# Two edits to a two-layer attention trunk: where 64-query products stand in the first layer, and how many rows the second layer's rotary low-part product uses

## The chip, the core and the metric

The kernel runs on one core of a Trainium2 chip. The metric is the device time of one execution in microseconds (us); lower is better. Three runs of the kernel before took 1453.0, 1454.13 and 1455.13 us, a median of 1454.13 us. A profile of one execution stands beside them.

The engines are named as in the profile: PE is TensorE's matmul, PEld its weight load, DVE is VectorE, ACT is ScalarE, POOL is GpSimd, SP is SyncE, which issues the weight transfers.

## What is computed

The input is x with 256 tokens of 2048 elements, float32. Two layers follow each other, each `x <- LayerNorm(alpha * x + out_proj(mixer(x) * silu(z)))`.

- Layer 1 mixes with three groups of 16 heads of 128 dims. Group 0 is a causal band over the last 128 tokens. Groups 1 and 2 attend with strides 4 and 16. Queries and keys carry rotary embeddings, and the three groups share one softmax.
- Layer 2 is latent attention: queries and keys/values come from latents of rank 512. Each of 16 heads has scores from two parts, a 128-dim part of its own and a 64-dim rotary part whose key is shared by all heads: `s = q_nope . k_nope + q_pe . k_pe`, causal, then softmax and values.

## The kernel before, in words

**Precision.** Most products run on operands split in two float32r parts, hi and lo, with lo = x - hi. `mm3` (lines 294 to 299) adds three products into one accumulator: hi by hi (L297), hi by lo (L298) and lo by hi (L299). The split of the weights is ACT's copy on L174 (`whi`) and DVE's subtraction on L175 (`wlo`), from tiles `raw` that SP loads on L155. Each weight block is used for 256 tokens and never again; four `whi` and four `wlo` half-blocks and three `raw` blocks are in flight. The large projections, tile `acc`, are the bulk of all matmuls.

**Order.** The loop bodies give a list of projection steps, and `run_slots` puts attention tasks behind given steps. The tile framework's planner then fixes the order on each engine, from a simulated timeline: where an instruction is not ready in that simulation, later work in program order is put in front of it. The order on each engine is fixed when the kernel is built.

**Layer 1.** Eight pairs of heads; each has 20 projection steps of 24 matmuls. In each, `scores(p, h)` runs for two heads, h = 0 behind step 13 and h = 1 behind step 15. For each of two query blocks qb of 128 queries it takes a PSUM tile `t`, fills columns 0 to 255 with group 0's scores by `mm3` (128 queries by 256 keys), and columns 256 to 383 with groups 1 and 2: tokens are permuted so that each class of 64 tokens attends within itself, so these are four products of 64 queries by 64 keys, in plain float32, each on the 64 output partitions of its class (L439). Each float32 product shows as two records. Then `softmax` (L357 to L360) runs on DVE and ACT over the tile, and `turn_p` transposes it some steps later. `qf`, the operand of L439, is copied out of PSUM by ACT on L404, after the transposes behind step 12.

**Layer 2.** Four quads of four heads. `scores_b(c, h)` fills one PSUM tile per head with the scores of both query blocks, 128 keys for the first and 256 for the second (`SEG`). For each block it issues `mm3` on the 128-dim parts and then two rotary products. The rotary operands are laid on both halves of the partitions: `qp` holds q's hi part on partitions 0 to 63 and its lo part on 64 to 127, and both `kp[0]` (hi) and `kp[1]` (lo) hold the same 64 rows of the key twice. L751 multiplies all 128 rows of `qp` with `kp[0]`, which gives (q hi + q lo) by k hi; L752 multiplies rows 0 to 63 alone with `kp[1]`, which gives q hi by k lo. Softmax follows on DVE and ACT, and `turn_pb` transposes the probabilities on L761 in a later task.

Of the kernel before, what the change touches and what calls it, by code (L numbers as in the profile page):

```python
# [38 lines left out]
SUB = 4          # k tiles of 128 that share one step of a wide projection chunk  # L39
CAP = SUB * 512  # elements per partition of one weight block  # L40

# token order of the first layer's attention: p = (t % 4) * 64 + (t % 16) // 4 * 16 + t // 16
# [3 lines left out]
class Plan:  # L46
    """The order in which weight blocks are stored and used. A block is [128, kts, n]."""
# [6 lines left out]
    def add(self, kts, n, pick):  # L54
        """pick(weights) gives the block's [kts * 128, n] columns."""
        self.blocks.append((self.size, kts, n))
        self.make.append(pick)
        self.size += P * kts * n
        return len(self.blocks) - 1
# [70 lines left out]
def trunk(ctx: ExitStack, tc: tile.TileContext, plan, ids, wall, xt, x, pos, freqs, mask_a, mask_b, rmst, ln, out):  # L130
    nc = tc.nc
# [12 lines left out]
    # ---------------------------------------------------------------- weights, in order of use  # L144
# [50 lines left out]
    # ---------------------------------------------------------------- x, transposed  # L195
# [17 lines left out]
    # ---------------------------------------------------------------- constants  # L213
# [20 lines left out]
    def rope_tables():  # L234
        pt = const.tile([P, 4], I32, name="pt")
        nc.gpsimd.dma_start(pt, pos)
        fr = const.tile([P, NA + NB], F32, name="fr")
        nc.gpsimd.dma_start(fr, bass.AP(tensor=freqs.tensor, offset=freqs.offset, ap=[[0, P], [1, NA + NB]]))
        with tc.tile_pool(name="tab", bufs=1) as tab:
            pf = tab.tile([P, 4], F32, name="pf")  # L240
            nc.vector.tensor_copy(pf, pt)
            ang = tab.tile([P, NT], F32, name="ang")
            part = tab.tile([P, 2, NT], F32R, name="part")
            acc = tab.tile([P, 2, NT], F32, name="acc")
            rd = tab.tile([P, 2, NT], F32, name="rd")
            for i, (a, n, f) in enumerate(((0, NA, 0), (NA, NA, 0), (2 * NA, NB, NA), (2 * NA + NB, NB, NA))):
                nc.vector.tensor_scalar(ang[:, a:a + n], fr[:, f:f + n], pf[:, i:i + 1], None, op0=ALU.mult)
            nc.vector.tensor_copy(part[:, 0], ang)
            nc.vector.tensor_sub(part[:, 1], ang, f32(part[:, 0]))

            def fraction(dst, src):
                """dst = src less the nearest whole number"""
                r = rd if len(src.shape) == 3 else rd[:, 0]
                nc.vector.tensor_scalar(r, src, MAGIC, None, op0=ALU.add)
                nc.vector.tensor_scalar(r, r, MAGIC, None, op0=ALU.subtract)
                nc.vector.tensor_sub(dst, src, r)

            # angle / (2 pi) in parts of 12 bits, each product exact and reduced to its fraction of a turn
            turn = [0x28BE60DB9391054A, 0x7F09D5F47D4D3770]
            bits = (turn[0] << 64) | turn[1]  # 1 / (2 pi) as a binary fraction of 128 bits  # L260
            cs = [float(bits >> (128 - 14)) * 2.0 ** -14]
            for i in range(1, 5):
                cs.append(float((bits >> (128 - 12 * (i + 1) - 2)) & 0xFFF) * 2.0 ** (-12 * (i + 1) - 2))
            for i, c in enumerate(cs):
                if i < 3:
                    pr = acc if i == 0 else tab.tile([P, 2, NT], F32, name="pr", tag="pr")
                    nc.vector.tensor_scalar(pr, f32(part), c, None, op0=ALU.mult)
                    fraction(pr, pr)
                    if i:
                        nc.vector.tensor_add(acc, acc, pr)  # L270
                else:  # under half a turn for any int32 position
                    nc.vector.scalar_tensor_tensor(acc, f32(part), c, acc, op0=ALU.mult, op1=ALU.add)
            si = acc[:, 0]
            nc.vector.tensor_add(si, si, acc[:, 1])
            fraction(si, si)
            co = acc[:, 1]
            nc.vector.tensor_scalar(co, si, 0.25, None, op0=ALU.add)
            fraction(co, co)
            w = 6.283185
            av = lambda t: t[:, :2 * NA].rearrange("p (t n) -> p t n", n=NA)  # L280
            bv = lambda t: t[:, 2 * NA:].rearrange("p (t n) -> p t n", n=NB)
            for v, c_t, s_t in ((av, cosA, sinA), (bv, cosB, sinB)):
                nc.scalar.activation(c_t, v(co), AF.Sin, scale=w)
                nc.scalar.activation(s_t[:, :, 1], v(si), AF.Sin, scale=w)
                nc.vector.tensor_scalar(s_t[:, :, 0], s_t[:, :, 1], -1.0, None, op0=ALU.mult)

    # ---------------------------------------------------------------- shared pieces
# [6 lines left out]
    def mm3(o, a, b, start, stop):  # L294
        """o += a.T @ b for operands in two exact parts; the parts' product lo x lo is below float32."""
# [9 lines left out]
    def power(dst, src, mul, eps):  # L305
        """dst = (src * mul + eps) ** -0.5"""
        nc.gpsimd.tensor_scalar(dst, src, mul, eps, op0=ALU.mult, op1=ALU.add)
        nc.gpsimd.tensor_tensor(dst, dst, mhalf.to_broadcast(list(dst.shape)), op=ALU.pow)

    def slots_wide(name, n, src, total=KT, step=SUB, tb_outer=False, evac=None):  # L310
        """One projection chunk: token-major [128 tokens, n] for both token blocks, as a list of steps."""
# [26 lines left out]
    def rope(dst, src, heads, half, c_t, s_t, tmp):  # L338
        """dst = rope(src) for src [128, heads, 2, half] in PSUM; tables [128, half] and [128, 2, half]."""
# [7 lines left out]
    def silu(dst, e):  # L347
        """dst = dst / (1 + e), e = exp(-dst), not before the weights that were split last"""
# [5 lines left out]
    def softmax(dst, src, mask, scale, sums, tmp):  # L354
        """dst = exp(scale * (src + mask) - max), sums = its row sums."""
# [8 lines left out]
    def run_slots(slots, todo):  # L364
        """Interleave: after step i the tasks todo[i]."""
# [5 lines left out]
    # ---------------------------------------------------------------- layer A: dilated windows  # L371
# [3 lines left out]
    def layer_a():  # L375
# [30 lines left out]
        def evac_v(p, part):  # L406
            def f(tb, acc):
                if part == 0 and tb == 0:
                    # group 0's values; groups 1 and 2's side by side for each class of tokens (t % 4)
# [17 lines left out]
        def scores(p, h):  # L427
            qh, ql, qf = pair[p, "q"]
            if h == 0:
                pair[p, "s"] = ap.tile([P, 2, 2, 384], F32, name="s", tag="s")  # L430
                pair[p, "sum"] = ap.tile([P, 4], F32, name="sum", tag="sum", bufs=2)
            for qb in range(2):
                t = at_tile()
                q = slice(qb * P, (qb + 1) * P)
                mm3(t[:, 0:256], (qh[:, h, q], ql[:, h, q]), (qh[:, 2 + h], ql[:, 2 + h]), True, True)
                for c in range(2):
                    for g in range(2):
                        q = slice(qb * P + 64 * c, qb * P + 64 * c + 64)
                        nc.tensor.matmul(t[64 * c:64 * c + 64, 256 + 64 * g:320 + 64 * g], qf[:, g, h, q], qf[:, g, 2 + h, q],  # L439
                                         start=True, stop=True)  # L440
                i = 2 * h + qb
                softmax(pair[p, "s"][:, h, qb], t[:, 0:384], mask[:, qb], SCALE_A, pair[p, "sum"][:, i:i + 1], ap)
# [31 lines left out]
        def values(p, h):  # L474
# [12 lines left out]
            def nat(a):  # tokens back in their own order  # L487
# [38 lines left out]
    # ---------------------------------------------------------------- output projection and LayerNorm  # L526
    def norm(v, mean, rstd, shift, gb, mul):
        """v = (v - mean) * rstd * g + b, on the vector engine alone or on three with mul for the product"""
# [8 lines left out]
    def norm_rows(layer):  # L537
        """the layer's g and b for each quarter of a row, on every partition"""
# [8 lines left out]
    def out_layer(tag, todo, res, u, whole):  # L547
        """u = ALPHA * res + y @ w_out; whole(tb, q, mean, rstd, -mean * rstd) ends a quarter of a token block's row.
        The last 8 steps are token block 0's last columns and then token block 1's."""
# [18 lines left out]
        # blocks are stored in the order 0.0 1.0 0.1 1.1 0.2 1.2 0.3 1.3  # L568
# [33 lines left out]
    # the first steps of the output projection finish the last heads  # L602
# [4 lines left out]
    # ---------------------------------------------------------------- layer B: latent attention  # L607
# [4 lines left out]
    shared = []  # one wide tile: first the latents, then gates' exponentials and values  # L612
# [64 lines left out]
    def heads_t(name, key, c, lat, parts_tag):  # L677
        """[128 dims, 4 heads, 256 tokens] in parts, weights stationary."""
# [33 lines left out]
    def turn_qp(c):  # L712
        """each head's rotary queries, [hi; lo] on the two halves of the partitions"""
# [25 lines left out]
    SEG = ((0, 128), (128, 256))  # columns of a head's scores, by query block  # L739

    def scores_b(c, h):
# [4 lines left out]
        for qb, (a, n) in enumerate(SEG):  # L746
# [3 lines left out]
            # (q hi + q lo) * k hi in one product, k's hi part being on both halves  # L750
            nc.tensor.matmul(o, qp[:, h, q], kp[0][:, 0:n], start=False, stop=False)  # L751
            nc.tensor.matmul(o, qp[0:64, h, q], kp[1][0:64, 0:n], start=False, stop=True)  # L752
# [117 lines left out]
# bits of 1 / 10000 ** (arange(0, dim, 2) / dim) in float32, for dim = 128 and dim = 64  # L870
# [16 lines left out]
def _constants():  # L887
# [3 lines left out]
    for qb in range(2):  # L891
        d = q[qb * P:(qb + 1) * P] - k
        mask_a[qb][:, 0:256][(d >= 0) & (d <= 128)] = 0.0
        for c in range(2):  # groups 1 and 2: keys of the query's own class
# [39 lines left out]
```

## Time and profile before

| | |
|---|---|
| median of 3 runs | 1454.13 us (1453.0 to 1455.13) |
| profiled execution, first to last instruction (its span) | 1453.4 us |
| granted TensorE clock, mean over the span | 0.993 |
| PE busy | 1426.5 us, 98%, 7346 matmul records |
| PEld busy | 1205.6 us, 83% |
| DVE busy | 915.8 us, 63% |
| ACT busy | 681.2 us, 47% |
| HBM traffic | 250.73 MB read, 174 GB/s over the span |

The profile gives no time of its own for the profiled execution beside its span. The span is 0.7 us under the median of the runs.

How to read it: busy time is the time in which an engine had an instruction under way. A matmul's record covers its whole way through the array, so successive matmuls overlap, and the distance from one start to the next says more than the length of a record. A weight load (PEld) belongs to the matmul of the same line that follows it. The timeline merges neighbours of the same kind into one row with their count.

### The profile page before, as it was taken

Reading aid. Unit: us, or ns where it says so; the run is one execution under the profiler, and the core shown is the slowest. Engines: PE = TensorE matmul, PEld = TensorE weight load, DVE = VectorE, ACT = ScalarE, POOL = GpSimd, SP = SyncE. Lnnn points to the kernel's source line nnn. Section 1 sums busy time; section 2 is a strip of 40 time slices with the busy share of each in tenths; the row PEclk is TensorE's granted clock in tenths of the full one; section 3 lists DMA queues with packets and bytes.
Section 4 is the critical chain, followed back from the end, with each engine's and each line's share of the span. In section 5 each row is a group of like instructions: output and inputs, shape, how many; then the busy total and the mean of one; then the engine's idle time right before and its main releaser. Section 6 shows DMA issues by size and latency. Waiting matters only on the chain.

```text
span 1453.4 us, 18499 instructions
## 1 busy us (share of the span) xinstructions
PE 1426.5 (98%) x7346; PEld 1205.6 (83%) x7346; DVE 915.8 (63%) x1435; ACT 681.2 (47%) x969; POOL 37.2 (3%) x46
## 2 busy tenths in 40 slices
PE   7999999999999999999999999999989999999996
PEld 5888888888888888888888888888889889889886
DVE  7656664765665666476566566645665687578655
ACT  5445445444444544544444454454335555555431
POOL 0000000000000000000000000000040000000002
PEclk9999999999999999999999999999989999999998
DMA  8545454455455554555455555446735544345552
GB/s 293 183 174 174 174 175 174 174 174 174 174 174 174 174 174 174 175 174 174 174 175 174 174 175 174 174 174 224 249 124 176 175 173 145 131 159 156 192 180 81
DMA packets 38982, 254.02 MB, mean 175 GB/s; under 512 B 4336, under 2 KB 5104, under 8 KB 10608
## 3 DMA queue, kind: packets, MB, share of 16 engines
q1 hardware_dynamic: 37504, 248.00, 49.3%
q0 software_dynamic: 1392, 4.84, 1.1%
q8 instruction: 57, 0.93, 0.3%
q14 instruction: 29, 0.24, 0.0%
HBM read 250.73 MB, written 2.10 MB: 174 GB/s over the span
## 4 chain that ended last, share of the span: by engine, by line
PE 97%; DVE 1%; POOL 1%; DMA 1%; issue 0%; ACT 0%; SPq 0%; POOLq 0%; DVEq 0%; ACTq 0%
PE acc L297 29%; PE acc L298 29%; PE acc L299 29%; PE at L398 1%; PE at L439 1%; PE o L483 1%; PE at L297 1%; PE o L778 1%; PE at L455 1%; PE at L752 1%; DMA raw<-in_wall 1%; PE at L298 1%; PE at L299 1%; PE at L761 0%; DVE wlo L175 0%
## 5 line engine op out<-in xcount | busy, mean ns | idle before, releaser
L175 DVE TENSOR_TENSOR wlo<-raw,whi 128x1024 fp32r<-128x1024 f32 (+2 forms) x470 | 565.4, 1205 | 434.4 <-ACT whi L174 434.2
L174 ACT CAST whi<-raw 128x1024 fp32r<-128x1024 f32 (+2 forms) x470 | 484.1, 1035 | 589.6 <-PE acc L299 520.4
L297 PE MATMUL acc<-whi,xh 128*128 128x512 f32 x1280 | 505.4, 396 | 7.1 <-ACT whi L174 7.0
L298 PE MATMUL acc<-wlo,xh 128*128 128x512 f32 x1280 | 505.1, 395 | 1.7 <-DVE wlo L175 1.7
L299 PE MATMUL acc<-whi,xl 128*128 128x512 f32 x1280 | 500.9, 391 | 0.0
L297 PEld LDWEIGHTS acc<-whi,xh 128*128 128x128 f32 x1280 | 241.2, 189 | 59.2 <-ACT whi L174 8.2
L298 PEld LDWEIGHTS acc<-wlo,xh 128*128 128x128 f32 x1280 | 241.5, 189 | 49.5 <-DVE wlo L175 2.6
L299 PEld LDWEIGHTS acc<-whi,xl 128*128 128x128 f32 x1280 | 241.6, 189 | 49.5
L299 PE MATMUL acc<-whi,x1l 128*128 128x512 f32 (+2 forms) x224 | 83.4, 372 | 0.6 <-DVE x1l L303 0.6
L297 PE MATMUL acc<-whi,x1h 128*128 128x512 f32 (+2 forms) x224 | 83.1, 376 | 0.6 <-ACT x1h L302 0.6
L298 PE MATMUL acc<-wlo,x1h 128*128 128x512 f32 (+2 forms) x224 | 83.2, 371 | 0.0
L298 PE MATMUL acc<-wlo,y2h 128*128 128x512 f32 (+1 forms) x160 | 55.7, 349 | 0.0
L297 PE MATMUL acc<-whi,yh 128*128 128x512 f32 (+1 forms) x160 | 55.6, 349 | 0.0
L299 PE MATMUL acc<-whi,y2l 128*128 128x512 f32 (+1 forms) x160 | 55.5, 349 | 0.0
L298 PE MATMUL acc<-wlo,yh 128*128 128x512 f32 (+1 forms) x160 | 55.4, 347 | 0.0
L299 PE MATMUL acc<-whi,yl 128*128 128x512 f32 (+1 forms) x160 | 55.4, 347 | 0.0
L297 PE MATMUL acc<-whi,y2h 128*128 128x512 f32 (+1 forms) x160 | 54.8, 350 | 0.0
L297 PEld LDWEIGHTS acc<-whi,x1h 128*128 128x128 f32 x224 | 43.5, 194 | 6.1 <-ACT x1h L302 0.8
L299 PEld LDWEIGHTS acc<-whi,x1l 128*128 128x128 f32 x224 | 43.5, 194 | 6.0 <-DVE x1l L303 1.0
L298 PEld LDWEIGHTS acc<-wlo,x1h 128*128 128x128 f32 x224 | 43.6, 195 | 5.0
L344 DVE TENSOR_TENSOR rb<-acc,sinA 128x256 f32<-128x256 f32 x96 | 35.8, 416 | 0.0
L345 DVE TENSOR_TENSOR r<-ra,rb 128x512 f32<-128x512 f32 x48 | 33.1, 690 | 0.8
(207 smaller groups left out, 1450.2 us busy)
## 6 DMA issues: line engine op xcount, KB each, us to landing
raw<-in_wall SPq DMA_DIRECT2D x221, 1024.0 KB, 4.9
raw<-in_wall SPq DMA_DIRECT2D x8, 832.0 KB, 4.5
gb<-in_ln POOLq DMA_DIRECT2D x8, 512.0 KB, 8.7
raw<-in_wall SPq DMA_DIRECT2D x4, 512.0 KB, 3.6
out<-u SPq DMA_DIRECT2D x8, 256.0 KB, 2.1
xr<-in_xt SPq DMA_DIRECT2D x3, 512.0 KB, 10.9
xres<-in_x SPq DMA_DIRECT2D x3, 512.0 KB, 4.8
raw<-in_wall SPq DMA_DIRECT2D x4, 256.0 KB, 6.2
```

Of the source, the lines that this page charges most:

```text
L174: nc.scalar.copy(hi[:, v], t[:, a:b][:, v])
L175: state["dve"] = nc.vector.tensor_sub(lo[:, v], t[:, a:b][:, v], f32(hi[:, v])).ins
L297: nc.tensor.matmul(o, ah, bh, start=start, stop=False)
L298: nc.tensor.matmul(o, ah, bl, start=False, stop=False)
L299: nc.tensor.matmul(o, al, bh, start=False, stop=stop)
L344: nc.vector.tensor_mul(b[:, :, s], src[:, :, 1 - s], s_t[:, s][:, None, :].to_broadcast([P, heads, half]))
L345: nc.vector.tensor_add(dst, a, b)
L398: nc.tensor.transpose(t[:, i * P:(i + 1) * P], r[:, i], ident)
L439: nc.tensor.matmul(t[64 * c:64 * c + 64, 256 + 64 * g:320 + 64 * g], qf[:, g, h, q], qf[:, g, 2 + h, q], start=True, stop=True)
L455: nc.tensor.transpose(t[:, i * P:(i + 1) * P], v[:, i * P:(i + 1) * P], ident)
L483: nc.tensor.matmul(o[:, q], v12[:, c, d], t12[:, q], start=False, stop=c == 3)
L752: nc.tensor.matmul(o, qp[0:64, h, q], kp[1][0:64, 0:n], start=False, stop=True)
```

## The change

Two edits; the rest of the diff takes out comments. In layer 1, `scores` takes both query blocks' PSUM tiles first and issues both `mm3` products, then all eight 64-query products, then both softmaxes; the instructions are the same ones in another order. In layer 2, L752's product runs over all 128 rows of `qp` and `kp[1]`, which adds q lo by k lo to the sum.

```diff
@@ def scores(p, h):
+            ts = [at_tile() for _ in range(2)]
             for qb in range(2):
-                t = at_tile()
                 q = slice(qb * P, (qb + 1) * P)
-                mm3(t[:, 0:256], (qh[:, h, q], ql[:, h, q]), (qh[:, 2 + h], ql[:, 2 + h]), True, True)
+                mm3(ts[qb][:, 0:256], (qh[:, h, q], ql[:, h, q]), (qh[:, 2 + h], ql[:, 2 + h]), True, True)
+
+            for qb in range(2):
                 for c in range(2):
                     for g in range(2):
                         q = slice(qb * P + 64 * c, qb * P + 64 * c + 64)
-                        nc.tensor.matmul(t[64 * c:64 * c + 64, 256 + 64 * g:320 + 64 * g], qf[:, g, h, q], qf[:, g, 2 + h, q],
-                                         start=True, stop=True)
+                        nc.tensor.matmul(ts[qb][64 * c:64 * c + 64, 256 + 64 * g:320 + 64 * g], qf[:, g, h, q],
+                                         qf[:, g, 2 + h, q], start=True, stop=True)
+            for qb in range(2):
                 i = 2 * h + qb
-                softmax(pair[p, "s"][:, h, qb], t[:, 0:384], mask[:, qb], SCALE_A, pair[p, "sum"][:, i:i + 1], ap)
+                softmax(pair[p, "s"][:, h, qb], ts[qb][:, 0:384], mask[:, qb], SCALE_A, pair[p, "sum"][:, i:i + 1], ap)
@@ def scores_b(c, h):
             nc.tensor.matmul(o, qp[:, h, q], kp[0][:, 0:n], start=False, stop=False)
-            nc.tensor.matmul(o, qp[0:64, h, q], kp[1][0:64, 0:n], start=False, stop=True)
+
+            nc.tensor.matmul(o, qp[:, h, q], kp[1][:, 0:n], start=False, stop=True)
```

## Rows read from the trace of the kernel before

**Rows 1.** The page: PE's busy time, and the chain that ended last by engine.

```profile
PE 1426.5 (98%) x7346; PEld 1205.6 (83%) x7346; DVE 915.8 (63%) x1435; ACT 681.2 (47%) x969; POOL 37.2 (3%) x46
...
PE 97%; DVE 1%; POOL 1%; DMA 1%; issue 0%; ACT 0%; SPq 0%; POOLq 0%; DVEq 0%; ACTq 0%
```

**Rows 2.** Windows, most of each layer: length, then busy by engine, PEclk, DMA.

```profile
100.00:990.00 890.00, 890.00 (x4351) 737.06 (x4350) 539.31 (x781) 419.04 (x593) 0.00 (x0) 1.00 0.50 173
1185.00:1440.00 255.00, 255.00 (x1506) 222.47 (x1505) 173.42 (x364) 121.07 (x202) 5.49 (x7) 1.00 0.45 151
```

**Rows 3.** Waits, whole span: who waited for whom, total us, times, longest.

```profile
ACT whi L174 <- PE acc L299: 520.4, 350, 6.2
...
PEld at L439 <- issue: 3.0, 8, 0.4
```

**Rows 4.** PE's timeline, layer 1, `scores` with h = 1: start, length, instruction, count.

```profile
106.75 0.28 PE L299 MATMUL at<-qh,ql 128*128 128x256 f32 x1
106.96 0.46 PE L439 MATMUL at<-qf 128*64 128x64 f32 x8
107.35 0.39 PE L297 MATMUL at<-qh 128*128 128x256 f32 x1
...
107.90 0.46 PE L439 MATMUL at<-qf 128*64 128x64 f32 x8
108.29 0.50 PE L297 MATMUL acc<-whi,xh 128*128 128x512 f32 x1
108.62 0.40 PE L298 MATMUL acc<-wlo,xh 128*128 128x512 f32 x1
```

**Rows 5.** The same for `scores` with h = 0, from its second query block on.

```profile
94.63 0.33 PE L439 MATMUL at<-qf 128*64 128x64 f32 x2
94.89 0.50 PE L297 MATMUL acc<-whi,xh 128*128 128x512 f32 x1
...
95.80 0.45 PE L439 MATMUL at<-qf 128*64 128x64 f32 x6
96.18 0.50 PE L297 MATMUL acc<-whi,xh 128*128 128x512 f32 x1
96.51 0.39 PE L298 MATMUL acc<-wlo,xh 128*128 128x512 f32 x1
```

**Rows 6.** L752's matmuls, by source line: count, min/median/max ns, first and last.

```profile
L752 PE MATMUL at<-kpl,qp x32: 322/352/382, 1186.7 to 1367.3; 64*128 64x128 f32 x16, 64*128 64x256 f32 x16
```

**Rows 7.** PE's timeline, layer 2, the first `scores_b`.

```profile
1186.53 0.22 PE L751 MATMUL at<-kph,qp 128*128 128x128 f32 x1
...
1187.16 0.28 PE L298 MATMUL at<-knl,qnh 128*128 128x256 f32 x1
...
1187.40 0.28 PE L751 MATMUL at<-kph,qp 128*128 128x256 f32 x1
1187.61 0.38 PE L752 MATMUL at<-kpl,qp 64*128 64x256 f32 x1
1187.92 0.50 PE L298 MATMUL acc<-wlo,x1h 128*128 128x512 f32 x1
1188.25 0.40 PE L299 MATMUL acc<-whi,x1l 128*128 128x512 f32 x1
```

**Rows 8.** PEld's timeline in the same call: weight loads.

```profile
1187.28 0.19 PEld L751 LDWEIGHTS at<-kph,qp 128*128 128x128 f32 x1
1187.60 0.18 PEld L752 LDWEIGHTS at<-kpl,qp 64*128 64x128 f32 x1
```

**Rows 9.** PE's timeline, layer 2, the third `scores_b`, first query block.

```profile
1197.61 0.22 PE L297 MATMUL at<-knh,qnh 128*128 128x128 f32 x1
1197.67 0.28 PE L298 MATMUL at<-knl,qnh 128*128 128x128 f32 x1
...
1197.89 0.28 PE L751 MATMUL at<-kph,qp 128*128 128x128 f32 x1
...
1198.57 0.28 PE L298 MATMUL at<-knl,qnh 128*128 128x256 f32 x1
```

## The prediction, on record before the result was known

> **What bounds the kernel now.** I read the page first, then the windows of the two long stretches, the waits, and last PE's timeline around the two edits, start by start. The page says that PE is busy for 98% of the span, and that the chain that ended last runs over PE for 97% of it [rows 1]. The reader is to see in the windows that this is not an average: from 100 to 990 us and from 1185 to 1440 us PE is busy for every microsecond, at the full granted clock (share 1.00, the 2.4 GHz level), while DVE is at 61% and 68% and the DMA share at 0.50 and 0.45 [rows 2]. Nearly all of both edits' places lie in these two stretches. Of the waits, the largest of those that concern the weights is ACT waiting for PE: 520.4 us in 350 waits for PE's last product on a half-block, before it may split the next weights [rows 3]. So PE sets the pace and the weight path follows; a distance between two matmul starts that shrinks is time off the span, unless something behind it is late.
>
> Busy PE is not PE at its peak here. A 256-column matmul follows another at 0.12 us: two such steps take 0.24 us [rows 7]. A 512-column one I take at twice that, 0.24 us (an estimate). Around the 64-query products and around L752 the steps are longer, though no wait is shown. What these products share is that they use the array in another shape (128 rows by 64 columns, 64 by 128) than their neighbours. L751's weight load starts at 1187.28, 0.12 us before its matmul at 1187.40; L752's starts at 1187.60, with its matmul at 1187.61 [rows 7, 8]. I read this so: the load is not drawn ahead across a change of shape, and the array stands still for a moment on the way in and on the way out.
>
> **Layer 1, part by part.** There are 16 calls of `scores` (8 pairs, 2 heads), and none of their instructions goes away. Take h = 1 [rows 4]. From the last `mm3` product of the first block (106.75) to the second projection matmul behind the call (108.62) are 1.87 us: 0.21 into the first run of 64-query products, 0.39 for its 8 records up to the next matmul, 0.55 for that matmul, two more and the way into the second run, 0.39 for that run, and 0.33 for a projection step behind it. After the edit the second block's three `mm3` matmuls follow the first's at 0.12 each (0.36), then one way in (0.21), 8 records and the way out (0.39), 8 further records, and 0.33. The trace has no run of 16. From first record to the next matmul, runs of 2, 6 and 8 take 0.26, 0.38 and 0.39 us [rows 4, 5], so a further record costs between 0.13/6 = 0.022 and, with a whole run's cost spread over it, 0.39/8 = 0.049 us; I take 0.03, which is (0.38 - 0.26)/4, as the nearest pair without the first fill. Eight more are 0.24 us. Sum 1.53, saved 0.34 us a call (0.19 to 0.41 by the bounds).
>
> In the calls with h = 0 the planner cuts the second block's run after 2 of its 8 records and puts three projection matmuls in the gap [rows 5]; the waits list has the 8 such places [rows 3]. Why it cuts can be read from the code: the third record needs `qf` of the second token block, which ACT copies last. In the new order the same PE work comes before that record, so I expect the same cut, after 10 records. Up to the projection at 94.89 the old way takes 0.21 + 0.39 + 0.55 + 0.26 = 1.41, the new one 0.36 + 0.21 + 0.39 + 2 records at 0.03 = 1.02: 0.39 saved, the rest unchanged. Layer 1: 8 x 0.34 + 8 x 0.39 = 5.8 us (4.3 to 6.6).
>
> What moves beside it: the first block's softmax on DVE starts some 0.4 us later and the second tile is taken 0.4 us earlier, at no cost. The probabilities are needed five projection steps on, and a step is 24 matmuls of about 0.24, over 5 us. No DMA is issued by the moved steps, and SP's and POOL's queues are not touched.
>
> **Layer 2.** There are 32 products on L752, 16 with 128 columns and 16 with 256 [rows 6]. With all rows each has its neighbours' shape, so I give it their steps. Second query block (256 columns): L751 to L752 0.21, on to the next 0.31, that one's successor 0.33, in all 0.85 [rows 7]; as plain steps 0.12 + 0.12 + 0.24 = 0.48. Saved 0.37. That holds for the 9 calls that a projection follows. In the other 7 the transposes of L761 follow; there I count only 0.21 + 0.31 - 0.24 = 0.28. First block (128 columns): from L751 to the second matmul behind L752 there are 0.63 us where L751 follows a projection [rows 7] and 0.68 where it follows `mm3` [rows 9], 8 calls each. Plain steps between 128-column matmuls are 0.11 (1197.67 to 1197.89 is two), with 0.06 for the first behind a projection [rows 9]: 0.06 + 0.11 + 0.12 = 0.29 and 0.11 + 0.11 + 0.12 = 0.34. Saved 0.34 either way. Layer 2: 16 x 0.34 + 9 x 0.37 + 7 x 0.28 = 10.8 us. The low end leaves out the short first step in 8 calls (10.4), the high end gives the 7 calls before transposes what the 9 have (11.4). Twice the contraction rows cost nothing by the rows: L751, with 128, is a plain 0.12 step.
>
> Sum: 5.8 + 10.8 = 16.6 us. It is made against the profiled span of 1453.4 us, for which the profile gives no other time; the median of the runs is 0.7 us above it, which I carry over: 1454.1 - 16.6 = 1437.5 us.
>
> **What is late next.** Weights first: with four half-blocks in flight and PE the one waited for [rows 3], 1.1% less PE time is covered by DVE's idle third. Closer is the chain from scores over DVE and ACT to the transposes in layer 2: a call ends 0.7 us earlier, but where DVE is at work on a weight split, the softmax does not start earlier.
>
> **Rivals.**
> 1. The cut in the h = 0 calls heals. Then the stretch from 94.89 to 96.51 (1.62 us) becomes six records at 0.03, one step of 0.33 and three of 0.24, 1.23 us; 8 x 0.39 = 3.1 more are saved: 1434.4 us. For: the simulated time of the copy is not known. Against: the work before the cut is the same.
> 2. New waits in layer 2 eat half of its gain, because softmax is held up behind splits on DVE: 5.4 back, 1442.9 us. For: DVE is at 68% there. Against: a task usually stands a projection step behind the one that feeds it.
> 3. The planner undoes side by side, with one more cut in each of the 16 runs: 16 x 0.39 = 6.2 back, 1443.7 us. Against: in the calls with h = 1 it left both runs whole.
> 4. Slower, by the same mechanism gone far: a cut run costs 0.39, so from 43 further cuts in the merged runs all is lost, and four in each run (64, 25.0 us) give 1462.5 us. There are 7 places for a cut in each run of 8 products. Against: one cut in two calls is all that the rows have.
> 5. Slower, with weight loads laid bare: if L752's load had to wait until L751's matmul on the same rows has ended, its start would come 0.28 + 0.19 = 0.47 after L751's instead of 0.21, and the next one's 0.47 after it instead of 0.31: 32 x 0.42 = 13.4 more, less layer 1's 5.8: 1461.7 us. Against: the load of L751 takes 0.19 and its matmul follows 0.12 after the load's start, behind a full-row matmul [rows 7, 8]. The Trainium skill, "TensorE: Matmul & The Clock Gate", section "The mechanism" of Part 3, states the rule that would do this: a weight load overlaps running matmuls only when its row group is another one. The rows speak against it for full-row neighbours, and by that I give it little.
>
> **Chances.** Forecast 0.66, rival 1 0.14, rival 2 0.10, rival 3 0.06, rivals 4 and 5 0.02 each. About 0.2% (2.9 us) is what a measurement of this kernel can tell from no change. All but rivals 4 and 5 are faster by more; I keep 0.02 for a loss and a gain that cancel and 0.03 for slower, so 0.95 faster. The forecast with its bounds is 1436.1 to 1439.4; the range takes in rival 1 with a planner's order that differs by some 2 us, and rivals 2 and nearly 3: 1432.0 to 1443.5.
>
> **What would show it.** In the new trace, 16 runs of L439 start 0.21 behind an `mm3` matmul; 8 of them have 16 records and take about 0.63 us to the next matmul, 8 are cut at 10 records with the other 6 later, 24 runs in all where there were 40. L752 shows 128 rows, lies 0.11 to 0.12 behind L751, and its load starts with L751's matmul or before. From 1185 us to the end of the projections PE stays busy throughout. The forecast is wrong if PE shows waits there, if L752's steps stay above 0.2 us, or if the runs of L439 number 32 or more.

## The result and the profile after

Four runs of the changed kernel took 1437.19 to 1439.68 us, median 1438.36 us; four runs of the kernel before beside them had a median of 1453.96 us. The ratio is 0.9891 (95% interval 0.9879 to 0.9902): 15.6 us faster. The forecast was 1437.5 us in a range of 1432.0 to 1443.5.

The page after, in the places of [rows 1]:

```profile
PE 1408.6 (98%) x7346; PEld 1197.7 (83%) x7346; DVE 914.6 (64%) x1435; ACT 680.1 (47%) x969; POOL 37.3 (3%) x46
...
PE 96%; POOL 1%; DMA 1%; DVE 1%; ACT 0%; SPq 0%; issue 0%; POOLq 0%; ACTq 0%
```

PE has as many records as before and 17.9 us less busy time; DVE and ACT have lost 1.2 and 1.1 us. PE is still busy for 98% of the span, and the chain that ended last runs over it for 96%. The span is 1435.4 us, where it was 1453.4.

The windows of the two long stretches after (length, busy by engine in the order PE, PEld, DVE, ACT, POOL, then the granted clock, the DMA share and GB/s), for [rows 2]:

```profile
100.00:980.00 880.00, 880.00 (x4328) 730.82 (x4327) 534.00 (x773) 416.15 (x590) 0.00 (x0) 1.00 0.50 174
1178.00:1422.00 244.00, 244.00 (x1504) 218.45 (x1503) 172.88 (x363) 120.74 (x202) 5.49 (x7) 1.00 0.46 157
```

PE is busy for every microsecond of both, as before. In these stretches no wait of PE has come up in place of the time that went. The waits list after, for the first row of [rows 3], shows ACT waiting for PE nearly as often as before (348 times, not 350) and a little less long:

```profile
ACT whi L174 <- PE acc L299: 512.8, 348, 6.2
```

PE's timeline of layer 1 after, for [rows 4, 5]: first a call with h = 0, then one with h = 1, then the same place in the next pair (start, length, instruction, count). The edit has moved the lines: L439 is now L441.

```profile
92.46 0.28 PE L299 MATMUL at<-qh,ql 128*128 128x256 f32 x1
92.67 0.56 PE L441 MATMUL at<-qf 128*64 128x64 f32 x10
93.16 0.50 PE L297 MATMUL acc<-whi,xh 128*128 128x512 f32 x1
93.49 0.39 PE L298 MATMUL acc<-wlo,xh 128*128 128x512 f32 x1
93.72 0.40 PE L299 MATMUL acc<-whi,xl 128*128 128x512 f32 x1
94.05 0.45 PE L441 MATMUL at<-qf 128*64 128x64 f32 x6
...
105.36 0.28 PE L299 MATMUL at<-qh,ql 128*128 128x256 f32 x1
105.57 0.73 PE L441 MATMUL at<-qf 128*64 128x64 f32 x16
106.24 0.50 PE L297 MATMUL acc<-whi,xh 128*128 128x512 f32 x1
106.57 0.39 PE L298 MATMUL acc<-wlo,xh 128*128 128x512 f32 x1
...
226.05 0.73 PE L441 MATMUL at<-qf 128*64 128x64 f32 x16
```

The run with h = 1 is whole (16 records), the one with h = 0 is cut after 10 records, with 6 later; the 24 runs of the trace are 8 of each kind. From the run of 16 to that of the next pair are 120.48 us. Before, the same place came at 106.96 [rows 4] and next in this row of PE's timeline, 121.13 us later:

```profile
228.09 0.46 PE L439 MATMUL at<-qf 128*64 128x64 f32 x8
```

So a pair has become 0.65 us shorter. PE's timeline of layer 2 after, for [rows 7]: the first `scores_b` (L751 is now L754, L752 is L756), and the first products of the second and third quad.

```profile
1178.98 0.22 PE L754 MATMUL at<-kph,qp 128*128 128x128 f32 x1
1179.04 0.27 PE L756 MATMUL at<-kpl,qp 128*128 128x128 f32 x1
1179.15 0.33 PE L297 MATMUL at<-knh,qnh 128*128 128x256 f32 x1
1179.32 0.28 PE L298 MATMUL at<-knl,qnh 128*128 128x256 f32 x1
...
1179.55 0.28 PE L754 MATMUL at<-kph,qp 128*128 128x256 f32 x1
1179.67 0.28 PE L756 MATMUL at<-kpl,qp 128*128 128x256 f32 x1
1179.78 0.39 PE L298 MATMUL acc<-wlo,x1h 128*128 128x512 f32 x1
1180.02 0.39 PE L299 MATMUL acc<-whi,x1l 128*128 128x512 f32 x1
...
1228.88 0.22 PE L754 MATMUL at<-kph,qp 128*128 128x128 f32 x1
...
1280.60 0.22 PE L754 MATMUL at<-kph,qp 128*128 128x128 f32 x1
```

L756, with 128 rows, is a step like its neighbours: 0.06 to 0.12 behind L754, and the next matmul 0.11 behind it, where L752 had 0.21 in front and 0.31 behind [rows 7]. From the second quad to the third are 51.72 us. The same two rows of before lie 54.33 us apart:

```profile
1239.02 0.22 PE L751 MATMUL at<-kph,qp 128*128 128x128 f32 x1
...
1293.35 0.22 PE L751 MATMUL at<-kph,qp 128*128 128x128 f32 x1
```

From the first such product of one quad to that of the next the trace after is 2.58, 2.61 and 2.57 us shorter, and from the fourth quad's to PE's last projection matmul 2.65, in all 10.4 us. So by the trace the edits give 8 x 0.65 = 5.2 us in layer 1 and 10.4 in layer 2, 15.6 us in all. The medians differ by as much (1453.96 - 1438.36); with an interval of about 1.7 us to either side, that they agree to the tenth is luck.

### The profile page after: what moved, and what is told of

Same layout as the page of the kernel before. It is cut to its first block, busy times and chain, and to the rows that moved or that the text cites. A ratio compares the mean times of both kernels' runs of the same rounds, so it can differ in the third digit from the quotient of the medians.

```text
span 1435.4 us, 18499 instructions
## 1 busy us (share of the span) xinstructions
PE 1408.6 (98%) x7346; PEld 1197.7 (83%) x7346; DVE 914.6 (64%) x1435; ACT 680.1 (47%) x969; POOL 37.3 (3%) x46
## 4 chain that ended last, share of the span: by engine, by line
PE 96%; POOL 1%; DMA 1%; DVE 1%; ACT 0%; SPq 0%; issue 0%; POOLq 0%; ACTq 0%
PE acc L297 29%; PE acc L299 29%; PE acc L298 29%; PE at L398 1%; PE o L486 1%; PE at L441 1%; DMA raw<-in_wall 1%; PE o L782 1%; PE at L458 1%; PE at L297 1%; PE at L299 1%; PE at L298 1%; DVE wlo L175 0%; PE at L765 0%; PE o L297 0%; PE o L298 0%
## 6 DMA issues: line engine op xcount, KB each, us to landing
xr<-in_xt SPq DMA_DIRECT2D x3, 512.0 KB, 11.3
```

## The experiments

The theory: a run of products in another array shape costs PE a fixed time, on the way in and on the way out, whatever the products compute; each run fewer gives that time back, nothing else changes, and the two edits add up. The rivals are that the gain comes from another order of the planner (rival A), that the half-row product itself is slow rather than the visit to its shape (rival B), and that one of the edits alone carries all of it (rival C).

**Each edit alone.** The first kernel is the changed one with layer 2's product back on half the rows; the second is the kernel before with that one line changed.

```diff
# e1_layer1_only, against the kernel after
-            nc.tensor.matmul(o, qp[:, h, q], kp[1][:, 0:n], start=False, stop=True)
+            nc.tensor.matmul(o, qp[0:64, h, q], kp[1][0:64, 0:n], start=False, stop=True)
# e2_layer2_only, against the kernel before
-            nc.tensor.matmul(o, qp[0:64, h, q], kp[1][0:64, 0:n], start=False, stop=True)
+            nc.tensor.matmul(o, qp[:, h, q], kp[1][:, 0:n], start=False, stop=True)
```

> Layer 1's edit alone; layer 2's low-part product stays on 64 rows. Theory (each visit to another array shape costs a fixed time on PE, nothing else moves): 24 runs of 64-query products instead of 40, 0.65 us a pair of heads as in the trace with both edits, so 5.2 us off: about 1448.8 where before is 1454.0; layer 2's quads as long as before (54.1 to 54.5 us). Rival (the two gains hang together, for instance through the planner's order): far from 5.2, or layer 2's quads change too.

> Layer 2's edit alone; the order of the instructions on every engine is that of before, one operand pair is 128 rows high instead of 64. Theory: 0.34 us for each first and 0.28 to 0.40 for each second product, 2.6 us a quad, 10.4 us in all: about 1443.6; L752 lies 0.06 to 0.12 behind L751 and its weight load starts before the matmul ahead of it. Rival (the gain came from a changed order, not from the shape): no more than 2 us off, 1452 or above.

Layer 1 alone: 1448.29 us, ratio 0.9963 (0.9950 to 0.9977). Layer 2 alone: 1443.44 us, ratio 0.9922 (0.9910 to 0.9934). These two and the next two share runs of the kernel before, whose median was 1454.7 us. PE's timeline of the first, two pairs and then two quads:

```profile
105.11 0.73 PE L441 MATMUL at<-qf 128*64 128x64 f32 x16
...
225.59 0.73 PE L441 MATMUL at<-qf 128*64 128x64 f32 x16
...
1230.80 0.22 PE L754 MATMUL at<-kph,qp 128*128 128x128 f32 x1
...
1285.12 0.22 PE L754 MATMUL at<-kph,qp 128*128 128x128 f32 x1
```

A pair takes 120.48 us, as in the kernel after; the quad takes 54.32, within the rounding of the 54.33 of before. With layer 2's edit alone it is the other way round: a pair takes as long as before (106.83 to 227.95 from one call with h = 1 to the next pair's), and its quad is as short as that of the kernel after, 51.72 us, as two rows of PE's timeline show:

```profile
1235.12 0.22 PE L751 MATMUL at<-kph,qp 128*128 128x128 f32 x1
...
1286.84 0.22 PE L751 MATMUL at<-kph,qp 128*128 128x128 f32 x1
```

Each edit gives in its own layer what it gives beside the other, so they add up and rival C falls. The medians alone would not show this: they lie 6.4 and 11.3 us under that of before, 17.7 together where both edits gave 15.6, and each has an interval of nearly 2 us to either side; the 5.2 and 10.4 are read from the traces. With layer 2's edit alone the instructions stand in the same order as before on every engine, so that gain comes from the shape alone, and rival A falls for layer 2.

**The visit or the product.** Here layer 2 keeps as many products on half the rows as before, but those of the two blocks stand side by side: the second block's accumulation begins with its half-row product, the first block's ends with its own.

```diff
# e3_l2_64rows_paired, against the kernel before, in scores_b
+            if qb == 1:
+                nc.tensor.matmul(o, qp[0:64, h, q], kp[1][0:64, 0:n], start=True, stop=False)
-            mm3(o, ..., True, False)
+            mm3(o, ..., qb == 0, False)
-            nc.tensor.matmul(o, qp[:, h, q], kp[0][:, 0:n], start=False, stop=False)
-            nc.tensor.matmul(o, qp[0:64, h, q], kp[1][0:64, 0:n], start=False, stop=True)
+            nc.tensor.matmul(o, qp[:, h, q], kp[0][:, 0:n], start=False, stop=qb == 1)
+            if qb == 0:
+                nc.tensor.matmul(o, qp[0:64, h, q], kp[1][0:64, 0:n], start=False, stop=True)
```

> Layer 1 as before. Layer 2's low-part products stay on 64 rows, but the second query block's one is issued first in its sum, so that both blocks' products stand next to each other: 16 visits to the 64-row shape instead of 32, with as many 64-row products. Theory (the visit costs, not the product): the second product is a plain step of about 0.11 and 0.34 us a call are saved, 5.4 us in all: about 1448.6. Rival (a 64-row product is slow in itself): each still pays, within 1 us of before, 1454.

Measured 1449.72 us, ratio 0.9966 (0.9953 to 0.9978). PE's timeline of its first call, and the first products of its second and third quad:

```profile
1186.21 0.22 PE L753 MATMUL at<-kph,qp 128*128 128x128 f32 x1
1186.37 0.32 PE L755 MATMUL at<-kpl,qp 64*128 64x128 f32 x1
1186.53 0.33 PE L750 MATMUL at<-kpl,qp 64*128 64x256 f32 x1
1186.79 0.38 PE L297 MATMUL at<-knh,qnh 128*128 128x256 f32 x1
...
1237.44 0.22 PE L753 MATMUL at<-kph,qp 128*128 128x128 f32 x1
...
1290.49 0.22 PE L753 MATMUL at<-kph,qp 128*128 128x128 f32 x1
```

A quad takes 53.05 us. This quad is 1.28 us shorter than before, and the four together save 5.1 us (5.0 by the medians), against 10.4 with all rows: half the visits give back half the time, with as many half-row products as before. So the visit costs, and rival B falls. It fits less well in one place: behind the first half-row product the second starts 0.16 us later (1186.37 to 1186.53), not at a plain 0.11, and the saving is 0.3 us under the 5.4 expected.

**The planner's cut.** The first experiment here puts `scores` with h = 0 one projection step later in the kernel after, so that `qf` is there for the second token block too. The second goes one step on: both heads in one task, all four `mm3` first, then all 32 records of the 64-query products, then four softmaxes.

```diff
# e4_uncut, against the kernel after
-at(13, scores, p, 0)
+at(14, scores, p, 0)
# e5_heads_together, against the kernel after
-at(13, scores, p, 0)
-at(15, scores, p, 1)
+at(14, scores, p)
 # scores(p):
+both = [(h, qb) for h in range(2) for qb in range(2)]
+ts = [at_tile() for _ in both]
+for t, (h, qb) in zip(ts, both):
+    ...
```

> Both edits, and the scores of the first head of a pair stand one projection step later, so that the copy of their operand is done in the planner's simulation too and the run of 64-query products is whole: 16 runs with 16 records instead of 24. Theory: 0.39 us for each of the 8 cuts, 3.1 us off the changed kernel: about 1435.3 where that has 1438.4. Rival (a cut costs nothing that lasts, since the projection matmuls in it are work that comes anyway): 1438.4, same as the changed kernel.

> Both edits, and both heads of a pair in one call behind step 14: four tiles, all `mm3` products, then all sixteen 64-query products, then four softmaxes; 8 runs of 32 records instead of 16 runs of 16. Theory (each visit costs 0.32 to 0.41 us, whatever its length): 2.6 to 3.3 us less than with 16 runs, 1.4 us a pair less than before: about 1432.5 where the changed kernel has 1438.4. Rival (four tiles are all that the pool has, and four softmaxes in a row hold ACT and DVE: PE waits for a tile or for weights): PE shows idle time between 100 and 990 us, and the time is 1435.5 or above.

> The changed kernel itself on this chip, as a measure for the version with the heads together. Theory and rival: 1437 to 1440, each pair of heads 120.48 us as in its first trace, each quad 51.5 to 51.8.

The uncut kernel took 1435.62 us, ratio 0.9868 (0.9855 to 0.9882). The heads together took 1432.32 us, ratio 0.9850 (0.9836 to 0.9863); the kernel after, run again beside it on the same chip, 1438.29 us (ratio 0.9888, 0.9874 to 0.9901), 6.0 us more. The kernel before, in its runs beside these two, had a median of 1454.98 us. PE's timeline of the uncut kernel, a call with h = 0, the same pair's with h = 1, and the next pair's with h = 0:

```profile
100.65 0.73 PE L441 MATMUL at<-qf 128*64 128x64 f32 x16
...
107.70 0.73 PE L441 MATMUL at<-qf 128*64 128x64 f32 x16
...
220.72 0.73 PE L441 MATMUL at<-qf 128*64 128x64 f32 x16
```

Both runs are whole, and a pair takes 120.07 us (100.65 to 220.72), 0.41 less than in the kernel after: 3.3 us for the 8 cuts, where 3.1 were expected and the medians differ by 2.7. PE's timeline with the heads together, and the window of layer 1 below it:

```profile
98.33 1.20 PE L441 MATMUL at<-qf 128*64 128x64 f32 x32
99.46 0.50 PE L297 MATMUL acc<-whi,xh 128*128 128x512 f32 x1
...
217.97 1.20 PE L441 MATMUL at<-qf 128*64 128x64 f32 x32
```

```profile
100.00:980.00 880.00, 880.00 (x4339) 733.75 (x4337) 537.84 (x790) 418.34 (x598) 0.00 (x0) 1.00 0.50 176
```

One run of 32 records a pair, a pair of 119.64 us, and PE without a gap still, now with 11 more matmuls in the same 880 us. With 5, 3, 2 and 1 runs of 64-query products in a pair, the pair takes 121.13, 120.48, 120.07 and 119.64 us, with the same products throughout: 0.32, 0.41 and 0.43 us for a run fewer. So the price of a visit is near 0.4 us, and not quite the fixed time of the theory. This speaks against rival A for layer 1: the time follows the number of runs, whichever way the order was reached, and in the kernel after the distances around the runs alone make up the 0.65 us of a pair (the next section has them). The last kernel is the fastest of the three, by the pairs 3.4 us under the uncut one.

**Shape or number format.** One rival the experiments do not separate in layer 1: the 64-query products are plain float32 and their neighbours float32r, so each visit changes the number format together with the shape. In layer 2, L752 and its score neighbours are all float32r, and there only the rows change. The trace of the kernel before has plain float32 products over the whole array among float32r neighbours: the value products on L483. PE's timeline around one run of them, then PEld's rows of the weight loads of this run and of the 64-query run of [rows 4] (each row is eight loads and shows where the first starts):

```profile
154.43 0.28 PE L299 MATMUL o<-th,v0l 128*128 128x256 f32 x1
154.54 1.00 PE L483 MATMUL o<-t,v 128*128 128x64 f32 x8
155.36 0.36 PE L297 MATMUL o<-th,v0h 128*128 128x256 f32 x1
155.56 0.28 PE L298 MATMUL o<-tl,v0h 128*128 128x256 f32 x1
155.68 0.28 PE L299 MATMUL o<-th,v0l 128*128 128x256 f32 x1
```

```profile
154.43 0.98 PEld L483 LDWEIGHTS o<-t,v 128*128 128x128 f32 x8
```

```profile
106.96 0.32 PEld L439 LDWEIGHTS at<-qf 128*64 128x64 f32 x8
```

On the way in, the change of format alone costs nothing here: L483 starts a plain step (0.11 us) behind the product ahead, and its first load starts that much earlier still, with that product. The 64-query run starts 0.21 us behind, and its first load only with it. On the way out the format does cost something: the product behind L483 takes 0.20 us to its successor (155.36 to 155.56), where the next one takes 0.12. So of the 0.32 to 0.43 us of a visit in layer 1, some 0.08 may belong to the number format; for the rest these rows leave the shape. No run gave the 64-query products the neighbours' format. The rows also warn against the full shape as a cure for layer 1: eight such records take 0.82 us over the whole array, about 0.10 each, where a further one of 64 columns takes 0.03.

## Why the prediction was right

**The bound.** The forecast rested on PE being the pace-setter with nothing late behind it. Both windows after show PE busy throughout, so each distance that shrank came off the span. No transpose of layer 2 kept PE waiting for DVE or ACT: rival 2 is out.

**Layer 1: 5.8 us foretold, 5.2 measured.** The mechanism and the cut came as described: 24 runs in place of 40, entries at 0.21 us (105.36 to 105.57), 8 runs of 16 and 8 cut at 10 and 6. Rivals 1, 3 and 4 are out with that. The term that was mis-sized is the price of a further record. I added records at 0.03 us to the 0.39 of a run of 8 [rows 4]. The run of 16 takes 0.67 us to the next matmul (105.57 to 106.24), not 0.63, and that of 10 takes 0.49 (92.67 to 93.16), not 0.45. Among the long runs a record does cost 0.03 us: (0.67 - 0.49) / 6 from 10 to 16, and (1.13 - 0.67) / 16 from 16 to 32, where the run with the heads together takes 1.13 (98.33 to 99.46). So what was too low is the base, by 0.04: the run of 8 lies below the line of the longer ones. That is 0.04 in each of two calls, 0.73 - 0.08 = 0.65 a pair. Rival 1's price, 0.39 a cut, was right within 0.02 (0.65 became 1.06 us a pair when the cut healed); only its condition didn't hold.

**Layer 2: 10.8 foretold, 10.4 measured.** The three terms of the forecast add up to 10.73, so to 10.7 and not 10.8 (the 16.6 of both layers stands). The second block's two rotary products and the matmul behind them take 0.47 us (1179.55 to 1180.02) where 0.48 was worked out: 0.38 saved, not 0.37. The first block's take 0.34 (1178.98 to 1179.32), not 0.29: the first 256-column product starts 0.11 behind the 128-column one, but its successor 0.17 behind it, and not the plain 0.12 that I had put there. Behind `mm3` it is 0.40 for 0.34. The saving is 0.28 to 0.29 in each of the 16 calls and not 0.34, 0.9 us less. The 7 calls before transposes gave 0.34 each and not 0.28, since the step from the first transpose to the second got shorter too (0.17 to 0.11), which brings 0.4 back; the other 9 gave 0.01 more each. Together that is 0.4 us less, which is the miss within the rounding.

**The weight load.** PEld's row of L756 after, in the first call's second block:

```profile
1179.55 0.19 PEld L756 LDWEIGHTS at<-kpl,qp 128*128 128x128 f32 x1
```

L756's load starts at 1179.55, with L754's matmul on the same rows and 0.12 us before its own. That refutes rival 5. The Trainium skill, "TensorE: Matmul & The Clock Gate", section "The mechanism" of Part 3, lists as a rule that a load overlaps running matmuls only when its row group is another one, but also names a background weight buffer, for which a load is drawn ahead as well. For full-row neighbours the trace does not agree with the first as it is worded. Before, L752's load started with its matmul [rows 7, 8]. The Trainium skill, "TensorEngine Tiling (Array Packing)", section "Key Properties", says that a change of tiling mode drains the engine. The trace agrees in that each visit to another shape costs time, 0.32 to 0.43 us here. Whether the load or the matmul is what has to wait at the change was not told apart by these runs.

**The sum.** 15.6 us against 16.6, and from the median that was shown, 1454.1 - 15.6 = 1438.5. I had the profiled execution 0.7 us faster than the median; in all results each run's time is 1.8 us above its span (1437.19 beside 1435.4), so it was one of some 1455.2, 1.1 above the median. As the edits' worth is the same in each execution, subtracting from the median was sound, and the miss of 0.9 us is that of the sum. It did mislead elsewhere: the two profiled spans differ by 18.0 us, 2.4 more than the edits. The windows of the first 35 us (before, after, after again; same columns) show where some of that lies:

```profile
0.00:35.00 35.00, 26.18 (x92) 20.03 (x93) 25.70 (x46) 17.80 (x21) 3.07 (x11) 0.95 0.80 289
```

```profile
0.00:35.00 35.00, 25.77 (x98) 19.55 (x99) 26.11 (x46) 19.01 (x23) 3.07 (x11) 1.00 0.80 287
```

```profile
0.00:35.00 35.00, 26.29 (x91) 20.04 (x92) 25.47 (x46) 17.46 (x21) 3.08 (x11) 0.90 0.80 286
```

The same kernel got 98 matmuls done there in one execution and 91 in another, at a granted clock of 1.00 and 0.90 (1.00 is the 2.4 GHz level), and its spans were 1435.4 and 1438.1 us. About 1.4 us of the 2.4 arise at the start: the first matmul on L398 comes at 46.38 us before and at 45.00 after. Some 1.0 arises behind the LayerNorm between the layers: from the first projection matmul there to the first product of `qp` with `kp[0]` are 109.74 us before and 108.74 after, and 108.55 with layer 2's edit alone, though neither edit touches that code. There too the granted clock differs: over the first 33.2 us of that stretch it was 0.85, 0.88 and 0.90 in these three traces.

## What to carry to other kernels

Where PE is always busy, look at the distances between matmul starts and not at waits: a lone product of another array shape costs its entry and exit, so put such products side by side, or, where a few stand alone as in layer 2 and the operands allow it, let them use the neighbours' full shape with terms that do no harm. Count visits to a shape, not products; and let no planner cut such a run, by putting the task where its last operand is ready. Sum the parts from trace distances between like places, since two profiled spans can differ by 2 us more than the change is worth.

## What was not expected of the hardware

- A second product on half the rows follows the first at 0.16 us, a full-row one with the same columns at 0.11; no run looked into why.
- A 256-column product whose predecessors are 128-column ones holds its successor for 0.17 us, not 0.12, with no wait shown.
- At the end of a run of 64-query products the next projection step takes 0.33 us (106.24 to 106.57) where a plain one takes 0.23 (93.49 to 93.72), so part of a visit's price falls on the matmul behind it. Behind plain float32 products over the whole array that step is longer too, by 0.08 (L483 above).
